# Down projections of two gated MLPs by seven block products instead of eight, with accumulating DMAs for some subtractions and sums

## The chip, the core and the metric

The kernel runs on one core of one Trainium2 chip. The metric is the time of one execution on the device in microseconds. The traces come from one profiled execution; its span runs from its first instruction to its last.

## The reference

A small decoder of two layers over 512 positions and 1024 channels, all in float32. Layer 0 mixes tokens with a gated DeltaNet, layer 1 with sliding-window attention. Each layer ends with the gated MLP that the change is about (`D_FF` is 2816):

```python
def conv_gated_mlp(hn, w_up, conv_w, conv_b, w_down):
    u = causal_dwconv(hn @ w_up, conv_w, conv_b)      # width 3, depthwise
    gate, val = jnp.split(u, 2, axis=-1)
    return (jax.nn.silu(gate) * val) @ w_down

def reference(x, ...):
    ...
    for layer in range(DEPTH):                          # DEPTH = 2
        h = h + (gated_deltanet(...) if layer < 1 else sliding_window_sink_attention(...))
        h = h + conv_gated_mlp(rmsnorm(h, ffn_norm_w[layer]), ffn_w_up[layer], ffn_conv_w[layer],
                               ffn_conv_b[layer], ffn_w_down[layer])
    return rmsnorm(h, final_norm_w)
```

## The kernel before

All large products are made from split operands: every float32 matrix x is cut into a high part (x rounded to the type that the matrix engine takes, `F32R`) and a low part x - high, and a product of 128x128 weights with 128x512 activations is three matmuls into one PSUM bank: high times high, high times low, low times high (`mm3`). PE is the matrix engine, DVE the vector engine, ACT the scalar engine, POOL and SP the two others; SP starts nearly all DMAs.

Channels lie on the 128 partitions and the 512 positions along the free dimension. The residual stream `h` is eight tiles of 128x512 in SBUF, two neighbours beside each other. Weights come by `load_stage`: one DMA on SP's queue brings up to eight 128x256 blocks into one of two `stage` buffers, and `cast` turns a 128-column half of them into weights, the high part by a copy on ACT (`whi`), the low part by a subtraction on DVE (`wlo`). There are three buffers of each.

`ffn` runs an MLP in two halves, channel tiles 0 to 11 and 12 to 21 of the 22. In a half's **up stage** each pair of channel tiles takes two stages (gate weights, value weights) and four `up` tiles of 24 matmuls each: gate 0, value 0, gate 1, value 1. What follows a tile is, on DVE and ACT: scaling out of PSUM, a scaled copy, two shifted multiply-adds (the convolution); for the gate a Silu; for the value the product with the gate, whose split gives the activations of the down projection. In the half's **down stage** there are eight output tiles m of 128 channels, two to a pair m2 and so to a pair of stages; each is 12 x 3 (then 10 x 3) matmuls of 128x512 into one bank of tag `d`, and DVE adds the bank to `h[m]`. The last output tile of all is made by `final` in two halves of 256 positions, between the last normalisation's pieces.

The program is written through a framework that gives buffers out and puts each engine's instructions into one order, by priority and by its own estimates; a table by hand sets the order of layer 0's token mixer, before the part that changes. Each engine then runs its list strictly in order, and waits where an operand or a buffer isn't ready. POOL has nothing to do in `ffn`, and issues no DMA in the kernel before.

Of the kernel before, what the change touches and what calls it, by code (L numbers as in the profile page):

```python
# [17 lines left out]
P = 128  # L18
T = 512
NC = T // P  # L20
D = 1024
KD = D // P
# [4 lines left out]
DFF = 2816  # L27
NF = DFF // P
# [13 lines left out]
def kernel(  # L42
# [26 lines left out]
    nc = tc.nc  # L69
    V, S, G, PE, SP = nc.vector, nc.scalar, nc.gpsimd, nc.tensor, nc.sync  # L70
# [6 lines left out]
    def nm(s):  # L77
        cnt[0] += 1
        return f"{s}_{cnt[0]}"

    wpool = ctx.enter_context(tc.tile_pool(name="weights", bufs=1, side="right"))
    psum = ctx.enter_context(tc.tile_pool(name="ps", bufs=1, space=PSUM))
    BANKS = {"d": 3, "g": 2, "s": 2, "p": 1}
    main = ctx.enter_context(tc.tile_pool(name="main", bufs=1))
# [13 lines left out]
        "o": 2,  # L98
        "p6s": 1,
        "gr": 1,  # L100
    }
# [12 lines left out]


    def load_stage(w, r0, kt, c0):
        st = wpool.tile([P, 8, 256], F32, tag="stage", bufs=2, name=nm("stage"))
        SP.dma_start(
            st[:, :kt, :],
            w[r0 : r0 + kt * P, c0 : c0 + 256].rearrange("(k p) c -> p k c", p=P),  # L120
        )
        return st

    def cast(st, kt, half, m=P):
        hi = wpool.tile([P, 8, P], F32R, tag="whi", bufs=3, name=nm("whi"))
        lo = wpool.tile([P, 8, P], F32R, tag="wlo", bufs=3, name=nm("wlo"))
        src = st[:, :kt, half * P : half * P + m]
        S.copy(hi[:, :kt, :m], src)  # L128
        V.tensor_tensor(lo[:, :kt, :m], src, hi[:, :kt, :m].bitcast(F32), op=ALU.subtract)  # L129
        return hi, lo  # L130

    def mm3(ps, w, kt, xh, xl, first=True, last=True, m=P):
        hi, lo = w
        for k in range(kt):
            PE.matmul(ps, hi[:, k, :m], xh[k], start=first and k == 0, stop=False)  # L135
            PE.matmul(ps, hi[:, k, :m], xl[k][:], start=False, stop=False)  # L136
            PE.matmul(ps, lo[:, k, :m], xh[k], start=False, stop=last and k == kt - 1)  # L137
# [16 lines left out]
    first = wpool.tile([P, 8, 256], F32, tag="stage", bufs=2, name=nm("stage"))  # L154
# [78 lines left out]
    st = [{} for _ in range(4)]  # L233
# [52 lines left out]
    gr = row("gr", F32R)[:, :]  # L286
# [56 lines left out]
    nk = const([P, 8, NC], s="nk")  # L343
# [369 lines left out]
    for i, line in enumerate(ORDER):  # L713
        for word in line.split():
            a, n = word[0], [int(d) for d in word[1:]]
# [22 lines left out]
        "rstd": ["p6s"],  # L738
        "qh": ["rq"],
        "ql": ["S"],  # L740
    }
# [15 lines left out]
    for h2 in range(HV // 2):  # L757
        a, b = wide("G"), wide("L")
# [6 lines left out]
    h4 = main.tile([P, 4, T], F32, tag="Xg", bufs=1, name="h4")  # L765
    h22 = [pair("pz") for _ in range(2)]
    hT = [h4[:, m, :] for m in range(4)] + [h22[m // 2][:, m % 2, :] for m in range(4)]
    for m in range(KD):
        xr = r2("hsq")
        x3 = xr[:].rearrange("p (c e) -> p c e", c=NC)  # L770
        SP.dma_start(x3, x[0, :, m * P : (m + 1) * P].rearrange("(c p) e -> p c e", p=P))
        pt = bank("g")
        for c in range(NC):
            PE.transpose(pt[:, c * P : (c + 1) * P], x3[:, c, :], ident[:])
        S.copy(hT[m], pt[:])
    for m2 in range(KD // 2):
        sts = [load_stage(a_w_out[0], 1024 * u, 8, 256 * m2) for u in range(2)]
        for j in range(2):
            m = 2 * m2 + j
            ps = bank("d")  # L780
            for u in range(2):
                w = cast(sts[u], 8, j)
# [4 lines left out]
    def rstd_cols(h):  # L787
# [13 lines left out]
        V.reciprocal(rt[:], rt[:])  # L801
        return rt

    def rstd_rows(h):
        rt = rstd_cols(h)
        dg = r2("sum")
# [12 lines left out]
    def normed(h, off):  # L819
        xh, xl = [], []  # L820
        for k in range(KD):
            a, b = r2("xh", F32R), r2("xl", F32R)
            split_scaled(h[k], norm_c[:, off + k : off + k + 1], a, b)
            xh.append(a)
            xl.append(b)
        return xh, xl


    def ffn(l, h, last=False):
        wup, wdn = ffn_w_up[l], ffn_w_down[l]  # L830
        uh, ul = normed(h, NFFN + 8 * l)
        rs = rstd_rows(h)

        def tap(j, t):
            i = j * 2 * NF + t
            return fcw[l][:, i : i + 1] if i < 128 else onw_c[:, 4 * l + i - 128 : 4 * l + i - 127]

        def up(w, t, tag):
            ps = bank("d")
            mm3(ps[:], w, KD, uh, ul)  # L840
            u = r2("u")
            V.tensor_tensor(u[:], ps[:], rs[:], op=ALU.mult)  # L842
            acc = r2(tag)
            b = CB + 2 * NF * l + t
            S.activation(acc[:], u[:], AF.Identity, bias=norm_c[:, b : b + 1], scale=tap(2, t))  # L845
            for d in (1, 2):
                V.scalar_tensor_tensor(  # L847
                    acc[:, d:], u[:, : T - d], tap(2 - d, t), acc[:, d:], op0=ALU.mult, op1=ALU.add
                )
            return acc  # L850

        for t0, t1 in ((0, 12), (12, 22)):
            gh, gl = [], []
            for t in range(t0, t1, 2):
                if l == 0 and t == 6:
                    bias_rows()
                sg = load_stage(wup, 0, 8, t * P)
                sv = load_stage(wup, 0, 8, DFF + t * P)
                gp, lp = wide("G"), wide("L")
                for j in range(2):  # L860
                    a = up(cast(sg, 8, j), t + j, "ga")
                    S.activation(a[:], a[:], AF.Silu)  # L862
                    b = up(cast(sv, 8, j), NF + t + j, "va")
                    V.tensor_tensor(b[:], a[:], b[:], op=ALU.mult)
                    split(b[:], gp[:, j, :], lp[:, j, :])
                    gh.append(gp[:, j, :])
                    gl.append(lp[:, j, :])
            ku = (t1 - t0) // 2
            for m2 in range(KD // 2):
                sts = [load_stage(wdn, (t0 + u * ku) * P, ku, 256 * m2) for u in range(2)]  # L870
                for j in range(2):
                    m = 2 * m2 + j
                    ws = [cast(sts[u], ku, j) for u in range(2)]
                    if last and t1 == NF and m == KD - 1:
                        final(h, lambda ps, ts, u: down(ps, ws, ku, gh, gl, ts, u))
                        continue
                    ps = bank("d")
                    for u in range(2):
                        down(ps[:], ws, ku, gh, gl, slice(0, T), u)
                    V.tensor_tensor(h[m], h[m], ps[:], op=ALU.add)  # L880

    def down(ps, ws, ku, gh, gl, ts, u):
        us = slice(u * ku, u * ku + ku)
        a, b = [t[:, ts] for t in gh[us]], [t[:, ts] for t in gl[us]]
        mm3(ps, ws[u], ku, a, b, first=u == 0, last=u == 1)

# [67 lines left out]
    def attention(h):  # L954
# [173 lines left out]
```

## Time and profile before

| | |
|---|---|
| median of 3 runs | 1457.99 us (1455.2 to 1465.97) |
| profiled execution | 1458.21 us, its span 1456.4 us |
| mean granted clock of PE | 0.996 |
| busy in the span | PE 98%, weight loads 80%, DVE 65%, ACT 49%, POOL 1% |
| DMA | 152.71 MB, 105 GB/s on average |

"Busy" is a share of the whole span, and the stages differ. PE's matmuls overlap their neighbours by design, so that the time from start to start, not the duration of one, says what a matmul costs. The profile's waits name what an engine waited for; the idle time of an engine that nobody waits for costs nothing. Lines (L137) are those of the kernel before where a row is of it, and of the changed kernel in rows of the changed program.

### The profile page before, as it was taken

The numbers are of one execution on the slowest core, as the hardware profiler recorded it, in microseconds if no ns is written. First come the engines' busy times: TensorE is split into PE (matmuls) and PEld (weight loads), VectorE is DVE, ScalarE is ACT, GpSimd is POOL, SyncE is SP. The second block draws the span as 40 slices with busy tenths as digits, with TensorE's granted clock in tenths as the row PEclk, the third lists the DMA queues.
The fourth block names the chain that finished last, engine by engine and source line by source line (L and its number), as shares of the span: only waits on it lengthen the run. The fifth ranks groups of instructions, "written<-read, shape, count | busy, mean of one in ns | idle before, by whom it ended". The sixth has DMA issues, their size and how long they took to land.

```text
span 1456.4 us, 19545 instructions
## 1 busy us (share of the span) xinstructions
PE 1432.3 (98%) x7519; PEld 1163.6 (80%) x7519; DVE 953.5 (65%) x1661; ACT 718.9 (49%) x1406; POOL 20.1 (1%) x47
## 2 busy tenths in 40 slices
PE   7999999999999999999999999999999999999998
PEld 5778877888877788888888888877788888888887
DVE  5896885978844436776247765777757774366754
ACT  7764564656646424443224444578744443234433
POOL 1000000000000000000010000000000000000000
PEclk9999999999999999999999999999999999999999
DMA  5334254163366523232232234221132322322222
GB/s 154 92 99 112 78 171 119 59 189 110 98 189 209 163 87 108 69 114 87 87 116 91 83 95 130 89 79 44 58 105 69 116 83 86 122 87 87 94 73 94
DMA packets 163074, 152.71 MB, mean 105 GB/s; under 512 B 24165, under 2 KB 150694, under 8 KB 162982
## 3 DMA queue, kind: packets, MB, share of 16 engines
q1 hardware_dynamic: 160722, 151.27, 33.3%
q8 instruction: 59, 0.97, 0.3%
q10 hardware_dynamic: 2259, 0.20, 0.2%
q14 instruction: 34, 0.27, 0.1%
HBM read 134.65 MB, written 16.80 MB: 104 GB/s over the span
## 4 chain that ended last, share of the span: by engine, by line
PE 95%; DMA 3%; ACT 1%; DVE 1%; issue 0%; ACTq 0%; DVEq 0%; SPq 0%
PE d L135 27%; PE d L137 27%; PE d L136 26%; PE s L585 2%; PE p L1043 1%; PE s L600 1%; PE g L1038 1%; PE s L625 1%; PE p L608 1%; PE s L562 1%; PE p L555 1%; PE s L1013 1%; PE g L450 1%; PE g L671 1%; PE g L375 1%; DMA ol<-od 0%
## 5 line engine op out<-in xcount | busy, mean ns | idle before, releaser
L135 PE MATMUL d<-xh,whi 128*128 128x512 f32 x1192 | 475.8, 400 | 0.1
L137 PE MATMUL d<-xh,wlo 128*128 128x512 f32 x1192 | 473.3, 398 | 0.0
L136 PE MATMUL d<-xl,whi 128*128 128x512 f32 x1192 | 471.6, 396 | 0.0
L128 ACT CAST whi<-stage 128x1024 fp32r<-128x1024 f32 (+2 forms) x236 | 230.5, 979 | 337.6 <-PE d L136 318.6
L129 DVE TENSOR_TENSOR wlo<-stage,whi 128x1024 fp32r<-128x1024 f32 (+2 forms) x236 | 267.3, 1133 | 120.4 <-ACT whi L128 114.3
L137 PEld LDWEIGHTS d<-xh,wlo 128*128 128x128 f32 x1192 | 224.4, 188 | 50.5 <-issue 1.4
L136 PEld LDWEIGHTS d<-xl,whi 128*128 128x128 f32 x1192 | 224.3, 188 | 48.2 <-issue 1.2
L135 PEld LDWEIGHTS d<-xh,whi 128*128 128x128 f32 x1192 | 224.7, 188 | 46.1 <-issue 0.7
L842 DVE TENSOR_TENSOR sz<-d,p6s 128x512 f32<-128x512 f32 x58 | 40.0, 689 | 62.9 <-PE d L137 61.0
L227 DVE SCALAR_TENSOR_TENSOR acc<-d,cwc,acc 128x511 f32<-128x511 f32 (+2 forms) x96 | 70.7, 740 | 9.3 <-ACT acc L224 8.8
L862 ACT ACTIVATE dt<-dt 128x512 f32<-128x512 f32 x44 | 27.8, 632 | 83.5 <-DVE dt L847 83.5
L135 PE MATMUL d<-sy,whi 128*128 128x512 f32 (+1 forms) x148 | 57.6, 390 | 0.0
L137 PE MATMUL d<-sy,wlo 128*128 128x512 f32 (+1 forms) x148 | 57.5, 389 | 0.0
L135 PE MATMUL d<-kT,whi 128*128 128x512 f32 (+1 forms) x146 | 57.5, 396 | 0.0
L136 PE MATMUL d<-sy,whi 128*128 128x512 f32 (+1 forms) x148 | 57.0, 385 | 0.0
L137 PE MATMUL d<-kT,wlo 128*128 128x512 f32 (+1 forms) x146 | 57.0, 390 | 0.0
L136 PE MATMUL d<-qT,whi 128*128 128x512 f32 (+1 forms) x146 | 56.8, 389 | 0.0
L847 DVE SCALAR_TENSOR_TENSOR va<-sz,fcw,va 128x511 f32<-128x511 f32 (+1 forms) x58 | 43.4, 748 | 2.7 <-ACT va L845 1.7
L847 DVE SCALAR_TENSOR_TENSOR dt<-sz,fcw,dt 128x511 f32<-128x511 f32 (+1 forms) x58 | 43.4, 748 | 1.2 <-ACT dt L845 0.2
L842 DVE TENSOR_TENSOR zl<-d,p6s 128x512 f32<-128x512 f32 x30 | 20.7, 689 | 33.4 <-PE d L137 33.1
L507 DVE TENSOR_TENSOR sT<-sT,p6s 64x31 f32<-64x31 f32 (+15 forms) x124 | 40.9, 330 | 2.0
L501 DVE TENSOR_TENSOR p6s<-sN,sT 64x31 f32<-64x31 f32 (+15 forms) x124 | 40.9, 330 | 1.8
(377 smaller groups left out, 2116.8 us busy)
## 6 DMA issues: line engine op xcount, KB each, us to landing
stage<-in_ffn_w_up_dram SPq DMA_DIRECT2D x44, 1024.0 KB, 5.1
stage<-in_a_w_in_dram SPq DMA_DIRECT2D x23, 1024.0 KB, 5.4
stage<-in_ffn_w_down_dram SPq DMA_DIRECT2D x16, 768.0 KB, 4.3
stage<-in_ffn_w_down_dram SPq DMA_DIRECT2D x16, 640.0 KB, 4.1
stage<-in_a_w_out_dram SPq DMA_DIRECT2D x8, 1024.0 KB, 5.0
zd<-sz SPq DMA_DIRECT2D x16, 256.0 KB, 2.1
od<-o SPq DMA_DIRECT2D x16, 256.0 KB, 2.5
stage<-in_b_w_q_dram SPq DMA_DIRECT2D x4, 1024.0 KB, 5.0
```

Source lines behind the costliest of these rows:

```text
L128: S.copy(hi[:, :kt, :m], src)
L129: V.tensor_tensor(lo[:, :kt, :m], src, hi[:, :kt, :m].bitcast(F32), op=ALU.subtract)
L135: PE.matmul(ps, hi[:, k, :m], xh[k], start=first and k == 0, stop=False)
L136: PE.matmul(ps, hi[:, k, :m], xl[k][:], start=False, stop=False)
L137: PE.matmul(ps, lo[:, k, :m], xh[k], start=False, stop=last and k == kt - 1)
L227: V.scalar_tensor_tensor(acc[:, d:], ps[:, : T - d], col, acc[:, d:], op0=ALU.mult, op1=ALU.add)
L501: V.tensor_tensor(tv, N[:, s, s + 1 : 32].unsqueeze(2).to_broadcast([64, n, m]), Tm[:, s : s + 1, 0:m].to_broadcast([64, n, m]), op=ALU.mult,)
L507: V.tensor_tensor(Tm[:, s + 1 : 32, 0:m], Tm[:, s + 1 : 32, 0:m], tv, op=ALU.subtract)
L585: PE.matmul(x[:, si], t[:, i, cs], S0[:, si], start=True, stop=True)
L842: V.tensor_tensor(u[:], ps[:], rs[:], op=ALU.mult)
L847: V.scalar_tensor_tensor(acc[:, d:], u[:, : T - d], tap(2 - d, t), acc[:, d:], op0=ALU.mult, op1=ALU.add)
L862: S.activation(a[:], a[:], AF.Silu)
```

## The change

It has three parts.

**Seven products.** A pair of output tiles (m, m+1) and a pair of channel tiles (f0, f1) with the positions in two halves of 256 make a product of 2x2 blocks. `seven_products` computes it from seven block products instead of eight, by sums of blocks taken ahead (the scheme of Strassen and Winograd). On the side of the activations `forms` makes four sums for each pair of channel tiles and splits f1, a half of f0 and the four sums into high and low parts, kept in rows that other parts of the program have left, three new rows of tag `f`, and `form_rows` hands them out. On the side of the weights each stage gets four sums of 128 x (3 x 128) or 128 x (2 x 128) elements, in place in the stage, and 3 casts of the whole width and one of the half (`cast`, `cast_to`). The matmuls are 128x256. Four products of a pair m2 collect in banks a, b, c, d, are added to `h` from there, two of them (a and d) collect a further product each and are added once more, one of these into three quarters of the pair at once, and the seventh (bank e) into two quarters. A down stage's stages are split into parts u = 0 (three channel pairs) and u = 1 (three, or two in the second half). The first two pairs m2 are interleaved: part 0 of both, then part 1 and the rest of the first, then of the second. The last pair m2 of the whole kernel stays as it was, eight products, with `final`.

**A third stage.** `down_stage` takes turns among the two `stage` buffers and a third one of its own (`st3`, 128 x 6 x 256), which also serves `rstd_rows`.

**Accumulating DMAs.** The low part of the value weights in the up stages (22 of the 44 weight tiles of a layer) is no longer made by DVE: ACT writes -high into the `wlo` buffer with one more instruction, and a DMA issued by POOL adds the weights to it from DRAM (`cast_added`). The first of the four sums of each down stage is made the same way, by a DMA that adds one block of the stage's weights from DRAM to another (`G.dma_start(A21, ...)`). There are 44 of the first kind (128 x 8 x 128 floats, 512 KB in pieces of 512 bytes) and 30 of the second (192 or 128 KB). The space that POOL keeps for the DMAs' descriptors is cut from its default to 4096 bytes a partition.

```diff
+    def cast_added(st, src, half):
+        hi, lo = weights()
+        hs = slice(half * P, half * P + P)
+        S.copy(hi[:], st[:, :, hs])
+        S.activation(lo[:], hi[:].bitcast(F32), AF.Copy, scale=-1.0)
+        G.dma_start(lo[:], src[:, :, hs], accum_op=ALU.add)
+        return hi, lo
...
+    def cast_to(w, at, src):
+        n = src.shape[1]
+        hi, lo = [t[:, at : at + n, :] for t in w]
+        S.copy(hi, src)
+        V.tensor_tensor(lo, src, hi.bitcast(F32), op=ALU.subtract)
...
                 for j in range(2):
                     a = up(cast(sg, 8, j), t + j, "ga")
                     S.activation(a[:], a[:], AF.Silu)
-                    b = up(cast(sv, 8, j), NF + t + j, "va")
+                    b = up(cast_added(sv, tiles_of(wup, 0, 8, DFF + t * P), j), NF + t + j, "va")
                     V.tensor_tensor(b[:], a[:], b[:], op=ALU.mult)
-                    split(b[:], gp[:, j, :], lp[:, j, :])
...
+                sevens.append(forms(*f, rows, plain))
...
+                sts = [down_stage(src) for src in srcs]
+                if not (plain and m2 == KD // 2 - 1):
+                    todo.append(seven_products(sts, srcs, parts, sevens, h_pairs[m2], m2 % 2))
+                    if m2 == 1:
+                        for i in (0, 1, 0, 0, 1, 1):
+                            next(todo[i])
...
+    def forms(f0, f1, rows, plain):
+        B11, B12, B21, B22 = f0[:, HALF[0]], f0[:, HALF[1]], f1[:, HALF[0]], f1[:, HALF[1]]
+        ta, tb = r2("Ta"), r2("Tb")
+        V.tensor_tensor(ta[:, HALF[0]], B12, B11, op=ALU.subtract)
+        V.tensor_tensor(ta[:, HALF[1]], B22, ta[:, HALF[0]], op=ALU.subtract)
+        V.tensor_tensor(tb[:, HALF[0]], B22, B12, op=ALU.subtract)
+        V.tensor_tensor(tb[:, HALF[1]], B21, ta[:, HALF[1]], op=ALU.subtract)
...
+    def seven_products(sts, srcs, parts, sevens, hp, odd):
...
+        a, b, d, c = [bank(t)[:, 0:256] for t in ("d", "g", "s", "d" if odd else "p")]
+        for u in range(2):
+            A11, A12, A21, A22 = blocks(u)
+            nk, end = len(parts[u]), u == 1
+            G.dma_start(A21, srcs[u][:, 1 : 2 * nk : 2, P : 2 * P], accum_op=ALU.add)
+            w = cast(sts[u], 2 * nk, 0)
+            product(a, w, 0, "B11", u)
...
+            product(b, w, 1, "B21", u)
...
+            V.tensor_tensor(A11, A21, A11, op=ALU.subtract)
+            V.tensor_tensor(A12, A12, A11, op=ALU.subtract)
+            w = cast(sts[u], 2 * nk, 1)
+            product(d, w, 0, "T1", u)
...
+            product(c, w, 1, "T4", u)
...
+            V.tensor_tensor(A22, A22, A11, op=ALU.subtract)
+            yield
+        e = bank("p" if odd else "g")[:, 0:256]
+        w4 = weights()
+        for u in range(2):
+            w = cast(sts[u], 2 * len(parts[u]), 0)
+            product(a, w, 0, "T2", u, first=False)
+            product(d, w, 1, "B22", u, first=False)
+            cast_to(w4, 4 * u, blocks(u)[3])
...
-    nc = _bacc.Bacc("TRN2", target_bir_lowering=False, num_devices=1)
+    nc = _bacc.Bacc("TRN2", target_bir_lowering=False, num_devices=1, dynamic_dma_scratch_size=4096)
```

Three places show how the order of the instructions changes.

**ACT in an up stage**, first half of layer 0, at the value weights of a pair's first tile. Before: the high part's copy (L128), the scaled copy of an earlier tile (L845), Silu (L862), the next gate weights.

```order
L128 CAST whi_5527<-stage_5487 128x1024
L845 ACTIVATE dt_5442<-sz_5440,normc_101,fcw_371 128x512
L862 ACTIVATE dt_5442<-dt_5442 128x512
L128 CAST whi_5565<-stage_5485 128x1024
L845 ACTIVATE va_5478<-zl_5476,normc_101,fcw_371 128x512
```

In the changed program stand there:

```order
L137 CAST whi_5552<-stage_5514 128x1024
L870 ACTIVATE dt_5453<-sz_5451,normc_101,fcw_371 128x512
L138 ACTIVATE wlo_5553<-whi_5552 128x1024
L889 ACTIVATE dt_5453<-dt_5453 128x512
L129 CAST whi_5589<-stage_5512 128x1024
```

The negated high part (L138) is new. It stands behind the scaled copy of an earlier tile (L870), which waits for DVE's scaling of that tile; the DMA on POOL can start only after L138.

**DVE where the first down stage begins**, after the last up tile (its product with the gate is L864 before, L891 now). Before: low parts of the weights of two stages and the sums into `h` (L880).

```order
L864 TENSOR_TENSOR va_6105<-dt_6069,va_6105 128x512
L141 TENSOR_TENSOR at_5963<-va_6105,at_5962 128x512
L129 TENSOR_TENSOR wlo_6167<-stage_6114,whi_6166 128x768
L880 TENSOR_TENSOR h_4560<-h_4560,d_6124 128x512
L129 TENSOR_TENSOR wlo_6213<-stage_6208,whi_6212 128x768
L129 TENSOR_TENSOR wlo_6217<-stage_6210,whi_6216 128x768
L880 TENSOR_TENSOR h_4560<-h_4560,d_6170 128x512
```

Now stand there the three remaining sums of the activations (L955 to L957), their four splits (L961), a sum of weights in the third stage (L1034), and then the first low part of the weights of part 1 (`wlo_6311`):

```order
L891 TENSOR_TENSOR va_6172<-dt_6135,va_6172 128x512
L130 TENSOR_TENSOR wlo_6287<-st_1017_6201,whi_6286 128x768
L955 TENSOR_TENSOR o_6177<-va_6172,o_6177 128x256
L956 TENSOR_TENSOR rq_6178<-va_6172,va_6099 128x256
L957 TENSOR_TENSOR rq_6178<-va_6172,o_6177 128x256
L961 TENSOR_TENSOR f_6184<-va_6172,f_6183 128x512
L961 TENSOR_TENSOR f_6187<-va_6099,f_6187 128x256
L961 TENSOR_TENSOR m_1013_6191<-o_6177,gr_6190 128x512
L961 TENSOR_TENSOR acc_6194<-rq_6178,m_1013_6191 128x512
L1034 TENSOR_TENSOR st_1017_6201<-st_1017_6201 128x3x128
L130 TENSOR_TENSOR wlo_6311<-stage_6199,whi_6310 128x768
```

All of L955 to L961 is ahead of `wlo_6311` in DVE's queue, so that PE's part 1 waits for it.

**DVE at the second pair of the down stage**, part 1, whose weights lie in `stage_6203`. Before, DVE at such a place had two low parts and one sum, as in the rows above. Now:

```order
L130 TENSOR_TENSOR wlo_6435<-stage_6203,whi_6434 128x768
L1011 TENSOR_TENSOR h_4560<-h_4560,g_6361 128x512
L1025 TENSOR_TENSOR stage_6203<-stage_6203 128x3x128
L1011 TENSOR_TENSOR h_4560<-h_4560,d_6257 128x256
L1026 TENSOR_TENSOR stage_6203<-stage_6203 128x3x128
L1011 TENSOR_TENSOR h_4560<-h_4560,g_6258 128x256
L130 TENSOR_TENSOR wlo_6461<-stage_6203,whi_6460 128x768
```

L1025 takes the sum that the accumulating DMA makes in `stage_6203`. The additions of two banks to `h` (L1011), L1026 and the next low part of weights are queued behind it.

More of the change, by code (lines that the diff above doesn't have):

```diff
@@ L100 @@
         "gr": 1,
+        "f": 3,
     }
@@ L740 @@
         "ql": ["S"],
+        "Ta": ["o"],
+        "Tb": ["rq"],
     }
@@ L850, in up @@
             return acc
-        for t0, t1 in ((0, 12), (12, 22)):
-            gh, gl = [], []
+        for t0, t1 in ((0, 12), (12, NF)):
+            plain = last and t1 == NF
+            rows = form_rows()
+            sevens = []
             for t in range(t0, t1, 2):
@@ new lines, with form_rows, parts, halves @@
+    HALF = [slice(0, 256), slice(256, 512)]
+    def form_rows():
+        for _ in range(len(YROLE)):
+            w = wide("G")
+            yield w[:, 0, :]
+            yield w[:, 1, :]
+        for tag in ("S", "S", "us", "f", "f", "f", "gr"):
+            yield row(tag, F32R)[:]
+        w = pair("m32", F32R)
+        yield w[:, 0, :]
+        yield w[:, 1, :]
+        yield row("acc", F32R)[:]
+    def forms(f0, f1, rows, plain):
[5 more added lines that the diff above has]
+        V.tensor_tensor(tb[:, HALF[1]], B21, ta[:, HALF[1]], op=ALU.subtract)
+        def parts(src, hi, lo):
+            S.copy(hi, src)
+            V.tensor_tensor(lo, src, hi.bitcast(F32), op=ALU.subtract)
+            return hi, lo
+        def halves(names, w):
+            return {n: [t[:, HALF[i]] for t in w] for i, n in enumerate(names)}
+        w1 = parts(f1[:], next(rows), next(rows))
+        out = {"f1": w1, **halves(("B21", "B22"), w1)}
+        if plain:
+            out["f0"] = parts(f0[:], next(rows), next(rows))
+            out.update(halves(("B11",), out["f0"]))
+        else:
+            r = next(rows)
+            out["B11"] = parts(B11, r[:, HALF[0]], r[:, HALF[1]])
+        out.update(halves(("T1", "T2"), parts(ta[:], next(rows), next(rows))))
+        out.update(halves(("T3", "T4"), parts(tb[:], next(rows), next(rows))))
+        return out
```

97 lines of the change are left out of this document (73 added, 24 removed).

## The prediction

> **What bounds the kernel now.** I read the page's head, its shares and its chain of waits first, then the busy time of each engine by stretches.
>
> ```profile
> span 1456.4 us, 19545 instructions
> PE 1432.3 (98%) x7519; PEld 1163.6 (80%) x7519; DVE 953.5 (65%) x1661; ACT 718.9 (49%) x1406; POOL 20.1 (1%) x47
> ...
> PE 95%; DMA 3%; ACT 1%; DVE 1%; issue 0%; ACTq 0%; DVEq 0%; SPq 0%
> ```
>
> The profiled execution took 1458.2 us, 1.8 us more than its span and 0.2 us from the median of the three runs, so the sum below is made against 1458.2. The chain that ended last is PE for 95%. The first row below is an up stage (layer 0, first half), the second the down stage behind it, the third a stretch of layer 1; columns are PE, PE's weight loads, DVE, ACT and POOL busy, then the granted clock.
>
> ```profile
> 553.00:684.00 131.00, 131.00 (x571) 106.62 (x570) 93.38 (x120) 58.75 (x73) 0.00 (x0) 1.00 0.28 87
> 684.00:750.00 66.00, 66.00 (x290) 54.13 (x290) 23.55 (x28) 14.55 (x17) 2.36 (x5) 1.00 0.33 104
> 1200.00:1300.00 100.00, 100.00 (x438) 82.07 (x437) 45.73 (x56) 28.02 (x34) 0.00 (x0) 1.00 0.30 98
> ```
>
> PE never idles in the MLPs, at full clock. DVE is busy 71% of the up stage and 36% of the down stage. So only two things count: how much PE time goes, and whether a wait opens on PE where there is none. 438 matmuls of 128x512 in 100 us is one per 0.2283 us.
>
> **What the seven products save on PE.** `final` runs 128x256 matmuls of the same kind today. The rows are the second of them and the last, 43 steps on:
>
> ```profile
> 1439.68 0.28 PE L136 MATMUL d<-nt,whi 128*128 128x256 f32 x1
> ...
> 1444.74 0.28 PE L137 MATMUL d<-kT,wlo 128*128 128x256 f32 x1
> ```
>
> 5.06 us / 43 = 0.1177 us, a little more than half of 0.2283. Before, 22 x 8 x 3 x 2 = 1056 matmuls belong to the down stages; the last pair's 60 stay, so 996 x 0.2283 = 227.4 us change. After, a pair m2 has 7 products x 6 (or 5) channel pairs x 3 matmuls: 4 x 126 and 4 x 105 in layer 0, 4 x 126 and 3 x 105 in layer 1, 1743 x 0.1177 = 205.2 us. **Saved: 22.2 us**, at most.
>
> **What DVE gets in a down stage.** Durations by shape (mean ns):
>
> ```profile
> L129 DVE TENSOR_TENSOR wlo<-stage,whi 128x768 fp32r<-128x768 f32 x32 | 30.7, 958 | 38.1 <-ACT whi L128 38.0
> L880 DVE TENSOR_TENSOR h<-h,d 128x512 f32<-128x512 f32 x16 | 11.0, 690 | 34.1 <-PE d L137 34.1
> L129 DVE TENSOR_TENSOR wlo<-gst,whi x1: 548/548/548, 18.2 to 18.2; 128x384 fp32r<-128x384 f32 x1
> L940 DVE TENSOR_TENSOR pz<-pz,d 128x256 f32<-128x256 f32 x2 | 0.8, 422 | 3.1 <-PE d L137 3.1
> L847 DVE SCALAR_TENSOR_TENSOR va<-sz,fcw,va 128x510 f32<-128x510 f32 x29 | 21.8, 751 | 1.0
> ```
>
> Neighbours overlap a little, as starts in the timeline show:
>
> ```profile
> 676.23 0.69 DVE L842 TENSOR_TENSOR zl<-d,p6s 128x512 f32<-128x512 f32 x1 [0.27 <-PE d L137]
> 676.87 0.96 DVE L129 TENSOR_TENSOR wlo<-stage,whi 128x768 fp32r<-128x768 f32 x1
> 677.81 1.54 DVE L847 SCALAR_TENSOR_TENSOR dt<-zl,fcw,dt 128x511 f32<-128x511 f32 x2
> ```
>
> So 512 elements cost 0.64 us, 768 cost 0.94, and with the same 0.05 off, 384 cost 0.50 and 256 cost 0.37. A pair m2 of a first half needs six low parts of 768, two of 384, six sums of 384 (the DMAs make the other two), five additions of 256 to `h`, one of 768, one of 512: 5.64 + 4.00 + 1.85 + 0.94 + 0.64 = 13.1 us, against 126 x 0.1177 = 14.8 us of PE. In a second half it is 11.7 against 12.4 us. Before it was about 5 us against 16.4. DVE has become nearly as long as PE, and the cover is thin wherever something comes late. I followed the changed order by hand at the first down stage; zero is the time at which PE could go on behind the last up matmul.
>
> *The beginning.* PE's result reaches DVE 0.2 us later than PE itself can go on (0.43 us from the start of a matmul to the addition that waits for it, less 0.23):
>
> ```profile
> 1430.71 0.39 PE L137 MATMUL d<-at,wlo 128*128 128x512 f32 x1
> ...
> 1431.14 0.69 DVE L880 TENSOR_TENSOR pz<-pz,d 128x512 f32<-128x512 f32 x1 [2.03 <-PE d L137]
> ```
>
> Then come, in DVE's queue up to `wlo_6311`: the scaling 0.64, a low part 0.94, two multiply-adds with a weight sum behind each 2.50, the product 0.64, a low part 0.94, three sums 1.11, four splits 2.29, a weight sum 0.50, and `wlo_6311` 0.94: 10.5, so it is there at 10.7 us. PE has part 0 of two pairs to do, 72 matmuls, and 8 high ones of part 1: 9.4 us. **PE waits 1.3 us** (none before: there a split of 0.69 us was all).
>
> *The second pair's part 1.* `stage_6203` reuses the buffer of `stage_6197`, whose last reader on DVE stands 5.4 us of work behind `wlo_6311`, at 16.1 us. Then the load, ACT's copy and DVE's low part:
>
> ```profile
> stage<-in_ffn_w_down_dram SPq DMA_DIRECT2D x16, 768.0 KB, 4.3
> acc<-in_x_dram SPq DMA_DIRECT2D x8, 256.0 KB, 2.9
> stage<-in_a_w_in_dram SPq DMA_DIRECT2D x2, 512.0 KB, 6.2
> stage<-in_ffn_w_up_dram SPq DMA_DIRECT2D x44, 1024.0 KB, 5.1
> ...
> L128 ACT CAST whi<-stage 128x768 fp32r<-128x768 f32 x32 | 26.8, 836 | 84.2 <-PE d L136 84.2
> L128 ACT CAST whi<-stage 128x1024 fp32r<-128x1024 f32 x172 | 180.4, 1052 | 193.0 <-PE d L136 178.4 <-DMA stage<-in_a_w_in_dram 4.2 <-issue 4.0
> L845 ACT ACTIVATE dt<-sz,normc,fcw 128x512 f32<-128x512 f32 x29 | 23.7, 817 | 0.8 <-DVE sz L842 0.6
> ```
>
> 16.1 + 4.3 + 0.84 + 0.94 = 22.2 us, while PE has finished the first pair and four matmuls near 21 us: **1.4 us** of waits with the small ones on the way. The accumulating DMA starts when the load has landed, at 20.4, and takes L_d; L1025 waits for it, and behind L1025 stand two additions, L1026 and `wlo_6461`, 2.7 us: 23.1 + L_d. PE is there at 24.8: it waits L_d - 1.7. Later pairs have 2 us or more in hand.
>
> *L_d* isn't in the trace: POOL issues no DMA. Nearest is the 256 KB row above, whose pieces are of 512 bytes too, 2.9 us; 192 KB would be 2.7. The destination is read as well, which at the 0.8 us that 256 KB more cost between the 768 and 1024 KB rows is 0.6; I add 0.3 for the writing of descriptors. Value 3.8, bounds 2.7 and twice 2.9. **So 2.1 us**, and 0.2 at the end of that pair: 5.0 us a down stage, **20 us for four**; one us of L_d more costs 4. The last pair of the kernel, whose weights queue behind the sums, gets 1.6 us.
>
> **What the up stages get.** DVE loses a low part of 1024 for each value tile, and gains the sums and more splits, in all within 1 us of the same per pair. No cover goes there: PE waited for nothing. ACT gains an instruction of 1.05 us, with 45% busy before. The new thing is the chain to the low part. Its buffer comes free when the tile three back is done; PE then has two tiles of 24 and two high matmuls to do, 50 x 0.2283 = 11.4 us. For the second value tile of a pair, DVE reaches the scaling that L870 waits for only 2.1 us after that (the sums and splits of the last pair stand in front), L870 takes 0.82 and L138 1.05, so the DMA goes off at 4.0 and has 7.4 us. The first value tile has 8.3. POOL's queue is in order, but the stage's sum in front of the last value tile is loaded long before.
>
> The DMA's duration, L_u, is the price that decides. The row of the same size and the same pieces, 512 KB of `in_a_w_in`, took 6.2 us; reading the destination too adds 1.6 at the rate above, descriptors 0.3: 8.1 us. Bounds: 2.9 (the 256 KB row) and twice 6.2 = 12.4. In each of 22 pairs of tiles PE waits for L_u less 7.4, once: 0.7 x 22 = **15 us**. By the Trainium skill, DMA: Bandwidth & Descriptors, section Anatomy of one DMA, a DMA that POOL issues takes 2.0 us plus its bytes at 436 GB/s, which for 512 KB would be an estimate of 3.2 us: no wait in the up stages, and a sum of 1458. The trace speaks against it only by the plain 6.2 us, and can't show the accumulation.
>
> **The sum:** 1458.2 - 22.2 + 20 + 1.6 + 15.4 = **1473 us**.
>
> **The rivals.**
> *The DMAs stay under their cover.* L_u of 7.4 or less: 1458, with L_d at its lower bound 1453, no change. For it: the 6.2 us row was taken with other loads in flight at the kernel's start, and 1024 KB land in 5.1. Against it: every reason above adds to the plain time.
> *The down stages hide their chains (faster).* If a stage's 5 us shrink to 1, as they would if ACT and DVE pieces overlap better than my list by hand and L_d is under 2.7, and L_u is under 7.4, it is 1442. For it: DVE's sums stay below PE's in every pair. Against: the 10.7 us chain is made of rows, and PE's cover there is 9.4 at most.
> *The up-stage DMAs are long (much slower).* With L_u at 12.4, (12.4 - 7.4) x 22 = 110 us in place of 15: 1568. It begins to decide at 9.5 us, 1504. POOL has to write some thousand descriptors for a DMA of 1024 pieces, which no row shows. By the Trainium skill, SBUF — State Buffer, section SBUF: two separate sides, DVE instructions that use two ports lock POOL out of writing descriptors, and a DMA of 0.62 us took 3.1; with 2.5 us more L_u it would be 1528 here. The rows of DVE in these stages are TENSOR_TENSOR and SCALAR_TENSOR_TENSOR, and that page has no two-port mode for the first.
> That the change doesn't do what it says, seven products and DMAs in place of DVE, is not open: the order has them.
>
> **How the numbers follow.** Forecast (L_u between 7.4 and 9.5, 1460 to 1504): 36%. Under cover, 1453 to 1460: 32%. Faster: 12%. Long DMAs: 20%. The range leaves out half of the faster case and the worst of the long one, where L_u is above 12: **1445 to 1562**. About 1%, 14.6 us, is what a measurement can tell from no change. Faster by over 1%: 12%. Within: the case under cover and the forecast's lower end, 37%. Slower: 51%.
>
> **What would show it.** PE's 128x256 matmuls at 0.118 us apart; PE waiting in up stages for DMA on `wlo` before every second value tile, none if L_u is below 7.4; the landing times of POOL's DMAs of 512 and 192 KB against 8.1 and 3.8; in each down stage one wait of about 1.3 us for DVE's `wlo` at the first part 1, and 2 us behind a DMA into a stage at the second pair. I am wrong if these DMAs are much shorter or longer, or if PE waits in the later pairs, where DVE's 13.1 of 14.8 us should be enough.

## The result, and the profile after

The changed kernel takes 1500.72 us (median of 4 runs, 1496.8 to 1504.46), the kernel before 1456.6: a ratio of 1.0285 (95% interval 1.0241 to 1.0329), 44 us slower by the medians. Its profiled execution has a span of 1502.5 us, 46.1 more than before. The page's head, shares and chain:

```profile
span 1502.5 us, 21864 instructions
PE 1438.9 (96%) x8266; PEld 1197.8 (80%) x8266; DVE 1059.1 (70%) x1974; ACT 810.1 (54%) x1554; POOL 126.6 (8%) x121
...
PE 83%; DMA 7%; DVE 5%; ACT 2%; issue 2%; DVEq 0%; POOL 0%; POOLq 0%; ACTq 0%; SPq 0%
```

PE's share of the chain has gone from 95 to 83%, and DMA and DVE have come in. The stages show where. The rows are, in this order, the first half of layer 0 (up, down), its second half (up, down), layer 1's mixer, and the second up stage of layer 1; columns as in the prediction.

```profile
556.45:691.77 135.32, 134.68 (x589) 109.24 (x588) 95.55 (x144) 72.31 (x96) 21.09 (x14) 1.00 0.70 146
691.77:757.45 65.68, 62.31 (x505) 60.88 (x504) 52.20 (x90) 25.80 (x36) 7.61 (x6) 0.97 0.46 120
757.45:880.53 123.08, 112.51 (x482) 91.55 (x481) 77.81 (x115) 58.85 (x77) 18.15 (x12) 0.96 0.63 129
880.53:939.57 59.04, 52.81 (x421) 50.03 (x420) 52.01 (x99) 30.43 (x49) 10.13 (x14) 1.00 0.40 104
939.57:1114.05 174.48, 171.54 (x932) 131.08 (x931) 126.60 (x318) 118.02 (x303) 5.69 (x9) 0.98 0.22 71
...
1313.34:1434.29 120.95, 112.45 (x483) 91.79 (x482) 78.00 (x115) 59.06 (x77) 19.44 (x13) 0.96 0.64 129
```

The same stretches of the kernel before:

```profile
547.07:681.52 134.45, 134.45 (x589) 109.32 (x588) 95.01 (x122) 59.58 (x76) 0.00 (x0) 1.00 0.29 91
681.52:747.45 65.93, 65.93 (x290) 54.09 (x289) 23.90 (x28) 15.16 (x19) 0.00 (x0) 1.00 0.33 104
747.45:857.31 109.86, 109.86 (x481) 90.14 (x480) 76.13 (x96) 46.61 (x59) 6.26 (x12) 1.00 0.29 93
857.31:912.25 54.94, 54.94 (x242) 45.07 (x241) 30.48 (x41) 22.18 (x32) 2.08 (x4) 1.00 0.38 117
912.25:1080.24 167.99, 167.99 (x932) 128.73 (x930) 123.45 (x313) 115.84 (x299) 0.00 (x0) 1.00 0.23 71
```

The first up stage, with twelve accumulating DMAs, loses 0.9 us; the second, with ten, loses 13.2. The down stages of the first halves come out even, that of layer 0's second half loses 4.1, and layer 1's mixer, whose instructions the change doesn't touch, loses 6.5. PE's waits from 480 us on, the longest in total (before, all of them together were under 1 us):

```profile
PE d L156 <- DMA wlo<-in_ffn_w_up_dram: 19.2, 3, 10.0
PE s L1006 <- ACT whi L129: 7.9, 4, 2.4
PE d L1008 <- DVE wlo L130: 6.0, 9, 1.0
PE g L796 <- DVE va L691: 2.8, 1, 2.8
PE d L154 <- ACT whi L129: 1.9, 1, 1.9
```

Only 3 of the 44 low parts made by DMA were waited for, two of them for 10.0 and 8.5 us. Both are the first value tile of a second half; the experiments call this place the entry. (The third wait, 0.6 us, is in layer 0's first half, behind a DMA that took 8.9 us.) The timeline at the entry of layer 0, engine by engine (SP, ACT, POOL, PE):

```profile
750.51 14.76 SPq L119 DMA_DIRECT2D stage<-in_ffn_w_up_dram  x4
760.66 1.05 ACT L137 CAST whi<-stage 128x1024 fp32r<-128x1024 f32 x1 [3.29 <-DMA stage<-in_ffn_w_up_dram]
761.61 1.05 ACT L129 CAST whi<-stage 128x1024 fp32r<-128x1024 f32 x1
762.56 1.06 ACT L138 ACTIVATE wlo<-whi 128x1024 fp32r<-128x1024 f32 x1
764.08 1.59 POOL L139 DMA_DIRECT2D wlo<-in_ffn_w_up_dram  x1 [17.93 <-PE d L156]
775.95 1.56 POOL L139 DMA_DIRECT2D wlo<-in_ffn_w_up_dram  x1 [10.29 <-issue]
765.22 0.40 PE L155 MATMUL d<-xl,whi 128*128 128x512 f32 x1
775.66 0.79 PE L156 MATMUL d<-xh,wlo 128*128 128x512 f32 x1 [10.04 <-DMA wlo<-in_ffn_w_up_dram]
776.25 0.63 PE L154 MATMUL d<-xh,whi 128*128 128x512 f32 x1
```

SP can issue the up stage's first load only at 750.5, 6.9 us before that stage begins at 757.5 (its first matmul). In the kernel before it was 732.8, 14.7 us ahead. The second load, of the value weights, goes out 4.4 us ahead in place of 10.5. The rows are SP in the kernel before, and what SP waited for before 750.5 in the changed one:

```profile
732.79 22.83 SPq L118 DMA_DIRECT2D stage<-in_ffn_w_up_dram  x4
...
SPq L119 <- DVE wlo L149: 11.8, 1, 11.8
```

L149 makes the low part of the weights for the seventh product, the last reader of a stage buffer. In layer 1 the gate weights come in time, and the value weights wait for L149 in the same way: their load goes out 7.3 us ahead in place of 10.5. There POOL's queue adds to it: L138 ends at 1314.4, but the DMA goes off at 1315.8, behind the DMA of a down stage's sum that had waited for its load until 1315.0.

At the entry of layer 0 the value weights land at 760.6, ACT's queue puts another copy in front of L138, and the DMA goes off at 764.1. It takes 11.5 us in place of its median of 6.4, and PE stands from 765.6 to 775.7. PE reached this tile 1.5 us after the DMA went off, so that 5 us of the 10.0 are the lateness, and 5 us that the DMA took 11.5 us and not 6.4. Then PE's matmuls are 0.43 us apart in place of 0.228, until 779.7: the granted clock has been halved.

```profile
770.00:780.00 10.00, 4.34 (x10) 3.46 (x11) 0.00 (x0) 0.00 (x0) 1.56 (x1) 0.50 0.81 133
```

That is 9 matmuls at 0.2 us more, 1.8 us on top of the wait. The Trainium skill (TensorE: Matmul & The Clock Gate, Part 1) describes this: the clock is halved after an idle window of about 3.4 us and comes back after a busy one. The trace agrees, with the granted clock of 0.50 and about 4 us of slow matmuls.

The accumulating DMAs themselves, KB each and median us to landing, then the spread of all 44 of the first kind (the other 15 and 8 are those of 192 KB):

```profile
wlo<-in_ffn_w_up_dram POOLq DMA_DIRECT2D x44, 512.0 KB, 6.4
stage<-in_ffn_w_down_dram POOLq DMA_DIRECT2D x15, 192.0 KB, 4.2
st<-in_ffn_w_down_dram POOLq DMA_DIRECT2D x8, 192.0 KB, 3.9
...
DMA to landing us min/median/max: 6.1/6.4/12.2
```

### The profile page after: what moved, and what is told of

The parts are those of the page before. It is cut to its first block, busy times and chain, and to the rows that moved or that the text cites. A ratio compares the mean times of both kernels' runs of the same rounds, so it can differ in the third digit from the quotient of the medians.

```text
span 1502.5 us, 21864 instructions
## 1 busy us (share of the span) xinstructions
PE 1438.9 (96%) x8266; PEld 1197.8 (80%) x8266; DVE 1059.1 (70%) x1974; ACT 810.1 (54%) x1554; POOL 126.6 (8%) x121
## 4 chain that ended last, share of the span: by engine, by line
PE 83%; DMA 7%; DVE 5%; ACT 2%; issue 2%; DVEq 0%; POOL 0%; POOLq 0%; ACTq 0%; SPq 0%
PE d L156 20%; PE d L154 20%; PE d L155 20%; DMA wlo<-in_ffn_w_up_dram 2%; DVE wlo L130 2%; PE s L604 1%; DMA stage<-in_ffn_w_down_dram 1%; PE d L1008 1%; PE p L1207 1%; PE s L619 1%; PE d L1006 1%; PE g L1202 1%; PE d L1007 1%; PE s L1008 1%; PE s L644 1%
## 5 line engine op out<-in xcount | busy, mean ns | idle before, releaser
L156 PE MATMUL d<-xh,wlo 128*128 128x512 f32 x1192 | 479.2, 403 | 20.7 <-DMA wlo<-in_ffn_w_up_dram 19.2
L155 PE MATMUL d<-xl,whi 128*128 128x512 f32 x1192 | 476.9, 401 | 0.0
L129 ACT CAST whi<-stage 128x1024 fp32r<-128x1024 f32 (+2 forms) x192 | 183.2, 958 | 243.2 <-PE d L155 158.0
L130 DVE TENSOR_TENSOR wlo<-stage,whi 128x1024 fp32r<-128x1024 f32 (+2 forms) x192 | 212.2, 1108 | 67.8 <-ACT whi L129 67.1
L139 POOL DMA_DIRECT2D wlo<-in_ffn_w_up_dram x44 | 69.8, 1587 | 651.0 <-ACT wlo L138 602.8
L867 DVE TENSOR_TENSOR sz<-d,p6s 128x512 f32<-128x512 f32 x58 | 40.0, 689 | 63.5 <-PE d L156 61.2
L137 ACT CAST whi<-stage 128x1024 fp32r<-128x1024 f32 x44 | 46.1, 1049 | 42.9 <-PE d L155 37.6
L138 ACT ACTIVATE wlo<-whi 128x1024 fp32r<-128x1024 f32 x44 | 46.2, 1051 | 0.2
L129 ACT CAST whi<-st 128x768 fp32r<-128x768 f32 (+1 forms) x30 | 23.7, 791 | 32.7 <-DMA st<-in_ffn_w_down_dram 10.4
L1017 POOL DMA_DIRECT2D stage<-in_ffn_w_down_dram x20 | 25.1, 1253 | 167.6 <-DMA stage<-in_ffn_w_down_dram 67.2
```

The costliest lines, as they stand in the source:

```text
L137: S.copy(hi[:], st[:, :, hs])
L138: S.activation(lo[:], hi[:].bitcast(F32), AF.Copy, scale=-1.0)
L139: G.dma_start(lo[:], src[:, :, hs], accum_op=ALU.add)
```

## The experiments

All were profiled, and compared with the kernel before on the same chip. The first table has their times, the second what the profiled execution of each spent in each stage, from the first matmul of a stage to the first of the next (us).

| | median us | ratio to before (95%) |
|---|---|---|
| changed | 1500.72 | 1.0285 (1.0241 to 1.0329) |
| the same again (e10) | 1498.41 | 1.0296 (1.0269 to 1.0324) |
| e1, two first value tiles on DVE | 1474.12 | 1.0126 (1.0090 to 1.0161) |
| e3, first down sums on DVE | 1473.2 | 1.0103 (1.0062 to 1.0145) |
| e4, no accumulating DMA | 1456.14 | 0.9989 (0.9976 to 1.0002) |
| e5, before + DMAs in the up stages | 1456.99 | 1.0006 (0.9982 to 1.0029) |
| e8, two loads held back | 1488.26 | 1.0207 (1.0180 to 1.0233) |
| e6, e4 + third stage last | 1456.2 | 0.9982 (0.9964 to 1.0000) |
| e9, e6 + one pair by eight products | 1450.14 | 0.9957 (0.9942 to 0.9972) |

| stage | before | changed | e10 | e1 | e3 | e4 | e5 | e8 | e6 | e9 |
|---|---|---|---|---|---|---|---|---|---|---|
| start to the first up tile | 547.1 | 556.5 | 544.6 | 543.5 | 554.5 | 549.7 | 544.2 | 545.6 | 544.8 | 553.6 |
| layer 0, up, first half | 134.4 | 135.3 | 134.4 | 135.4 | 134.9 | 134.4 | 134.4 | 135.1 | 134.4 | 134.4 |
| down, first half | 65.9 | 65.7 | 64.6 | 64.4 | 63.5 | 62.8 | 65.9 | 66.0 | 62.2 | 62.1 |
| up, second half | 109.9 | 123.1 | 122.4 | 111.2 | 118.9 | 110.8 | 109.9 | 118.6 | 109.9 | 109.9 |
| down, second half | 54.9 | 59.0 | 61.1 | 59.8 | 54.1 | 53.9 | 54.9 | 61.6 | 54.1 | 55.6 |
| layer 1's mixer | 168.0 | 174.5 | 174.7 | 174.3 | 173.9 | 173.9 | 168.0 | 174.7 | 174.0 | 168.0 |
| layer 1, up, first half | 133.7 | 133.7 | 133.7 | 133.7 | 133.7 | 133.7 | 133.7 | 133.7 | 133.7 | 133.7 |
| down, first half | 65.9 | 65.6 | 65.2 | 65.8 | 62.1 | 62.1 | 65.9 | 65.7 | 62.1 | 62.1 |
| up, second half | 109.9 | 121.0 | 124.8 | 111.6 | 115.8 | 109.9 | 109.9 | 118.8 | 109.9 | 109.9 |
| down and end | 66.7 | 68.2 | 71.0 | 69.8 | 66.1 | 66.0 | 66.7 | 68.7 | 66.1 | 66.1 |
| first up tile to the end | 909.3 | 946.1 | 951.9 | 926.1 | 923.0 | 907.6 | 909.4 | 942.9 | 906.3 | 901.8 |

**e1: the first value tile of each second half on DVE.**

```diff
-b = up(cast_added(sv, ..., j), NF + t + j, "va")
+early = t == 12 and j == 0
+wv = cast(sv, 8, j) if early else cast_added(sv, ..., j)
+b = up(wv, NF + t + j, "va")
```

> The changed kernel, but the low part of the first value tile of each MLP's second half (t = 12, j = 0, two tiles in the program) is again made by DVE; the other 42 stay with the accumulating DMA. Theory A (entries): in the up stages the DMAs cost time only where a second half begins, because there the value weights land late and the DMA then shares the DMA engines with the next stage's load (12 us for 6.4). The two waits of 10.0 and 8.5 us and the slow clock behind them, about 2.3 us each, go: 1500 - 23 = 1477 us, and both second up stages come back to about 110 us. Theory B (everywhere): the 28 MB more of DMA traffic and POOL's work slow the program in many places, and the waits only move to the second value tile: 1492 or more.

1474.12 us, and the second up stages 111.2 and 111.6 us: two of 44 DMAs cost nearly all that the up stages lost (1.3 and 1.7 us are left). The entry is the place, as theory A said; theory B is out.

**e3: the first sum of the down stages on DVE.**

```diff
-G.dma_start(A21, srcs[u][:, 1 : 2 * nk : 2, P : 2 * P], accum_op=ALU.add)
 w = cast(sts[u], 2 * nk, 0)
+V.tensor_tensor(A21, A21, A22, op=ALU.add)
```

> The changed kernel, but the first sum of each down stage (30 sums) is made by DVE, behind the first low part of its stage, and not by an accumulating DMA. Theory A: the wait of PE at the second pair's part 1 (1.9, 2.0, 1.6 and 2.4 us in the four down stages), which ACT's copy of the sum passes on, and the slow clock behind it (about 2 us) go: 12 to 15 us less, 1486 us. Rival (DVE is full): DVE gets 30 x 0.5 = 15 us more in stages where it is already 0.8 busy, so that as much is lost in waits for the low parts as is gained: 1500 us or more.

1473.2 us, twice the gain that was expected. In the second pair of a down stage of the changed kernel one sees the wait that theory A named (the rows are of POOL, DVE and PE):

```profile
711.93 1.27 POOL L1017 DMA_DIRECT2D stage<-in_ffn_w_down_dram  x1 [28.61 <-DMA stage<-in_ffn_w_down_dram]
716.07 0.56 DVE L1025 TENSOR_TENSOR stage<-stage 128x384 f32<-128x384 f32 x1 [2.31 <-DMA stage<-in_ffn_w_down_dram]
716.96 0.38 PE L1006 MATMUL s<-ktok,whi 128*128 128x256 f32 x1 [1.88 <-ACT whi L129]
```

That wait is gone in e3, and the four down stages together are 12.7 us shorter (258.5 to 245.8 by the table), close to the expected. The rest was not expected: without the sums' DMAs the last pair lets go of its buffers sooner (the up stage's first load is issued at 744.6, 8.3 us ahead of the stage, in place of 6.9), at layer 1's entry no sum stands in front in POOL's queue, and the waits at the entries fell too:

```profile
PE d L156 <- DMA wlo<-in_ffn_w_up_dram: 7.0, 3, 4.7
```

The sum on DVE did not make DVE the bound.

**e4: no accumulating DMA.** e3 with `cast` in place of `cast_added` everywhere.

> The changed kernel without any accumulating DMA: seven products and the third stage alone, all low parts and all sums on DVE. Theory A: the gains of the two other runs add up: 1500 - 23 - 14 = 1463 us, with up stages of 134 and 110 us as in the kernel before. Rival (DVE is full): in the up stages DVE had 71% before and gets the sums and splits beside its old low parts, and the waits for it make 1480 us or more.

1456.14 us, no different from before, and 7 us less than theory A's sum. The up stages are back to 134.4, 110.8, 133.7 and 109.9 us with all low parts on DVE, so DVE had room for them beside the new sums and splits. PE's waits from 480 us on, the first rows:

```profile
PE d L1008 <- DVE wlo L130: 3.6, 6, 1.0
PE d L154 <- ACT whi L129: 3.6, 2, 3.1
PE d L1006 <- ACT whi L129: 1.2, 3, 0.6
PE s L1008 <- DVE wlo L130: 1.1, 3, 0.4
```

So the DMAs cost 38.5 us from the first up tile on (946.1 less 907.6), and the seven products with the third stage alone gain 1.7 us of the 22.2 that PE has less to do. The four down stages are 8.6 us shorter than before. They lose the other 13.6 us in themselves: the rows with L1008 and L1006, 5.9 us of waits for weights, are theirs. Layer 1's mixer takes back 5.9 us, and the second up stage of layer 0 0.9.

**e5: the kernel before with the DMAs of the up stages alone.**

```diff
-b = up(cast(sv, 8, j), NF + t + j, "va")
+b = up(cast_added(sv, ..., j), NF + t + j, "va")
```

> The kernel before, with eight products as they were, and only the 44 low parts of the value weights by accumulating DMA (and the same space for descriptors as in the changed kernel). Theory A: the same entries show: two waits of about 9 us and the slow clock behind them, 1457 + 22 = 1479 us, nothing elsewhere. Theory B (everywhere): 1490 us or more. A third possibility: without the seven products the stage's buffers come free earlier at the entry, and the waits are half as long: 1467 us.

1456.99 us, and each stage as before. No theory had this. At its second up stage's beginning (744.5 us), SP and POOL:

```profile
729.85 43.54 SPq L118 DMA_DIRECT2D stage<-in_ffn_w_up_dram  x6
742.91 1.56 POOL L138 DMA_DIRECT2D wlo<-in_ffn_w_up_dram  x1 [76.08 <-ACT wlo L137]
...
DMA to landing us min/median/max: 6.2/6.5/7.4
```

The load is issued 14.6 us ahead of the stage, the DMA goes off before the stage begins, and none of the 44 takes over 7.4 us. The DMAs alone cost nothing. What differs at this place in the changed kernel is that the seven products read each stage buffer until the end of a pair, so that the loads behind it come late (SP's wait for L149 above).

**e8: the next loads held back at the entry.** POOL copies one element of the first low part into each of the next two stage buffers, so that their loads wait until the DMA has landed.

```diff
+def hold(c):
+    st = wpool.tile([P, 8, 256], F32, tag="stage", bufs=2, name=nm("stage"))
+    G.tensor_copy(st[:, 0, 0:1], first_lo[:, 0, 0:1].bitcast(F32))
+    SP.dma_start(st[:], tiles_of(wup, 0, 8, c + (t + 2) * P))
+    return st
...
```

> The changed kernel, but where a second half begins, the two stage loads of the next pair of channel tiles (t = 14) are held back until the accumulating DMA of the first value tile has landed: POOL copies one element of the low part into each stage buffer first. Theory (shared DMA engines): that DMA took 11.5 and 12.2 us in place of 6.4 because these two loads of 1024 KB ran beside it. Alone it takes 6.4 us, and the two waits of PE fall from 10.0 and 8.5 to about 5 and 3 us: 10 us less than the changed kernel, 1490 us. Rival (the DMA is long for a reason of its own at that place, such as work queued on POOL or engines writing to SBUF): it still takes 11 to 12 us and nothing changes, 1500 us.

1488.26 us. POOL and PE at the first entry, then POOL at the second:

```profile
753.40 1.59 POOL L139 DMA_DIRECT2D wlo<-in_ffn_w_up_dram  x1 [18.15 <-PE d L156]
760.19 0.30 POOL L889 COPY stage<-wlo 128x1 f32<-128x1 f32 x2 [5.20 <-DMA wlo<-in_ffn_w_up_dram]
759.98 0.80 PE L156 MATMUL d<-xh,wlo 128*128 128x512 f32 x1 [5.06 <-DMA wlo<-in_ffn_w_up_dram]
...
1305.62 1.26 POOL L1030 DMA_DIRECT2D st<-in_ffn_w_down_dram  x1 [19.80 <-DMA st<-in_ffn_w_down_dram]
1306.38 2.12 POOL L139 DMA_DIRECT2D wlo<-in_ffn_w_up_dram  x1
1313.57 0.79 PE L156 MATMUL d<-xh,wlo 128*128 128x512 f32 x1 [6.46 <-DMA wlo<-in_ffn_w_up_dram]
```

Without the two loads, the DMAs take 6.6 and 7.2 us from issue to PE's next matmul, not 11.5 and 12.2: the loads beside them made them long, as the theory said. The waits fell from 10.0 and 8.5 to 5.1 and 6.5 us. What is left is lateness. At the second entry it was more than expected, and there the DMA of a down stage's sum (L1030, here for the next down stage's first load) stands in front in POOL's queue, as it does in the changed kernel, and waits for that load until 1305.6. The two second up stages are 6.7 us shorter together; from the first up tile on, e8 is 3.2 and 9.0 us shorter than the two profiled executions of the changed kernel. The 12 us between the medians can't be placed closer than that.

**e6: e4 with the third stage last in every half.**

```diff
-if turns[0] % 3 == 0:
+if (turns[0] - 1) % 8 + 1 in (2, 5, 8):
```

> As the kernel without accumulating DMAs (e4, 1456 us), but the third stage takes the 2nd, 5th and 8th stage of every half, in place of every third one of the whole program, so that it always holds the last stage and both ordinary buffers come free earlier at the end of a half. Theory: the 6 us that the start of layer 1's mixer lost in all these kernels (a wait of 3.1 us for the copy of weights that landed late, and the slow clock behind it) go, and 1 us where layer 0's second half begins: 1450 us. Rival: the buffers are held as long, since the last stages are read to the end, and the place of the third stage doesn't matter: 1456 us.

1456.2 us. The second up stage is back to 109.9 us, but the mixer is as long as in e4, 174.0 us. The load came a little sooner (issued 3.4 us ahead of the mixer in place of 2.5), but PE still waits 2.1 us for ACT's copy and 1.2 us for DVE's low part. The theory was wrong on the mixer.

**e9: e6 with the last pair of layer 0's second half by eight products.**

```diff
-plain = last and t1 == NF
+plain = t1 == NF
```

The diff shows one line; the second output tile of that pair is also made like the first where `final` doesn't follow.

> As e6 (1456.2 us), but in layer 0 too the last pair of output tiles of the second half is made by eight products of 128x512, as it is in layer 1. Theory: the 6 us lost at the start of layer 1's mixer come from DVE, which is still at the last pair's additions and low parts when the mixer needs its first weights; eight products need 1.3 us more on PE, but less than half of DVE's work there, so that most of the 6 us come back: 1452 us. Rival: the wait is for the weights of the mixer, whose load comes late whatever DVE does, and the pair only costs its 1.3 us: 1457 us.

1450.14 us: faster than the kernel before by 0.43% (interval 0.28 to 0.58). The first 113 us of the mixer:

```profile
915.52:1028.25 112.73, 112.73 (x643) 85.57 (x642) 86.82 (x230) 83.54 (x219) 0.00 (x0) 1.00 0.24 77
```

The pair costs 1.5 us (54.1 to 55.6), and the mixer is back to 168.0 us, with PE busy without a gap in its first 113 us. By the stages e9 is 4.5 us shorter than e6 (906.3 to 901.8); the intervals of the two ratios still overlap. The first 5 us of the mixer, in e6 and in e9:

```profile
905.33:910.33 5.00, 1.81 (x8) 0.86 (x6) 5.00 (x9) 3.59 (x5) 4.07 (x8) 1.00 0.22 77
915.52:920.52 5.00, 5.00 (x27) 4.17 (x26) 3.18 (x5) 3.72 (x5) 0.00 (x0) 1.00 0.63 210
```

In e6 DVE is busy all the time and PE 1.8 us of 5; in e9 PE is busy all the time and DVE 3.2 us. The load of the mixer's second weights also went out sooner in e9, 11.3 us ahead in place of 3.4. So the loss came from this pair, by its work on DVE or its hold on the stage buffers; one run doesn't say how much was which.

**e10: the changed kernel once more.**

> The changed kernel once more, unchanged. Its profiled execution was 9.4 us behind the kernel before already at the first up tile, where both programs issue the same instructions; kernels run since then had that point between 543 and 555 us. Theory (scatter of the clock's dips in layer 0's mixer): the point lies somewhere between 543 and 557 us again, while the stages behind it repeat to within 2 us: 123, 59, 121 and 68 us for the second up stage, the second down stage, the last up stage and the end. Rival (the change itself slows the mixer): the point is at 555 us or later again.

1498.41 us. The first up tile starts at 544.6 us, not at 556.5: the 9.4 us that the first profile lost before the MLPs are scatter. The rows are 340 to 344 us of the kernel before and of the first profile of the changed one:

```profile
340.00:344.00 4.00, 4.00 (x29) 3.56 (x28) 4.00 (x7) 2.17 (x4) 0.00 (x0) 1.00 0.23 36
340.00:344.00 4.00, 4.00 (x22) 3.04 (x21) 1.53 (x3) 1.46 (x4) 1.09 (x2) 0.50 0.15 25
```

In this execution the clock fell to half in a stretch of small matmuls, where the other had all of it from 320 to 352 us (0.84 on average in this one). Not all stages repeat to within 2 us: the last up stage took 124.8 us for 121.0, the second down stage 61.1 for 59.0, and the end 71.0 for 68.2. The waits at the entries were 9.8 and 12.0 us this time, behind DMAs of 11.3 and 13.5 us.

## Why the prediction was wrong

The sum was 15 us above the profiled time of before; the medians are 44 apart. From the first up tile on, the first profile lost 36.7 us and the second 42.6. By the prediction's own terms, in the first profile:

- *PE's saving, -22.2 us.* Right. The 128x256 matmuls are 0.1177 us apart where nothing waits, 504 of them 59.3 us, and what a down stage takes beyond that are waits.
- *Four down stages, +20 + 1.6 us, so -0.6 with the saving.* Measured +5.0 with it. For the first halves 64.5 us was forecast each (65.9 less the saving of 6.4, and 5.0): 65.7 and 65.6, 64.6 and 65.2 in e10. The single waits came as predicted: 0.9 us for 1.3 at the first low part of part 1, and 1.9 us for 2.1 behind the DMA of the second pair's sum, with an L_d of 4.2 or 3.9 us for the 3.8 assumed. (2.7, 0.6 and 0.3 us, from which L_d was added up, make 3.6, not 3.8, and with it 19.2 us for four stages, not 20.) The 1.9 us were a wait for ACT's copy of the sum; DVE's queue behind the sum, which the prediction followed, added a wait of 0.07 us. Not in the sum was that the clock can fall behind such a cluster of waits:

```profile
720.00:724.00 4.00, 4.00 (x28) 4.00 (x28) 2.65 (x5) 1.46 (x3) 0.00 (x0) 0.76 0.27 87
```

  The second half of layer 0 was undersized: 9.6 us beyond its 420 matmuls (49.4 us), where 5.0 were put. DVE is busy 52 of its 59 us, and there are eight waits of 0.2 to 2.0 us.
- *The up stages, 0.7 us in each of 22 pairs, 15.4 us.* Measured 25.2 us: of the right order by chance, and **wrong in both parts**. L_u is 6.4 us, not 8.1, and so under the cover, the time from the DMA's start to PE's need: in the steady state there is no wait, and that rival was right there. The 0.3 us that L_u and L_d had for descriptors is in no run a figure of its own. By the Trainium skill's rule that the prediction weighed (DMA: Bandwidth & Descriptors, section Anatomy of one DMA) the estimate was 3.2 us; the measurement decides, at twice that. The step that failed is the cover: 7.4 and 8.3 us were worked out from the buffer three tiles back, for a pair in the middle of a stage, and used for every pair. In the middle they hold: from the DMA's issue to PE's first use the trace has 7.7 to 8.9 us there. Where a second half begins, a load of the stage is late, so that the cover is 1.5 us in layer 0 and 3.7 in layer 1, and the DMA runs beside two loads of 1024 KB and takes 11.5 and 12.2 us. The prediction had also set POOL's queue aside, since the sum in front of a value tile "is loaded long before"; in layer 1 it was not, which is 1.4 us of the lateness. Two waits and the slow clock behind them make most of the 13.2 and 11.1 us that these up stages lose. e5 shows that the DMA alone doesn't do it, e8 that the shared transfer is about half of the wait at the first entry, e1 that these two tiles are nearly all of it.
- *Layer 1's mixer, not in the sum.* 6.5 us. The prediction followed the order by hand at the first down stage and not past the last one. The last pair's work reaches into the mixer: e9 shows that it is this pair, and not whether by DVE's low parts and additions or by the late hold on the buffers.
- *Start to the first up tile.* 9.4 us of the first profile, -2.5 in the second: scatter.

"Later pairs have 2 us or more in hand" held for the first halves, where no later pair waits, and not for the second. The rival with long DMAs put its price on all 22 pairs, and none of the rivals had the entry as a place of its own.

## What to carry to other kernels

A cover that is worked out from the steady state doesn't hold at the seams: follow the first item of a stage from the moment its buffer comes free, through every queue, to the wait. Who holds a buffer longer delays a load two stages on, and an operation that got longer by a few us in a place with slack (e5) becomes a wait where the slack has gone. And a scheme that saves PE time by giving DVE more pays only where DVE has room: taking one of the fifteen pairs back to eight products turned no change (e6) into 0.4% faster.

## What the runs showed of the hardware

- An accumulating DMA of 512 KB in pieces of 512 bytes takes 6.4 us in the median; it took 8.9 and 9.4 us beside one load of 1024 KB and one of 768 KB, and 11.5 and 12.2 us beside two of 1024 KB. With those two held back it took 6.6 and 7.2 us (e8).
- POOL is busy for 1.57 us with each of these DMAs (median; 1.56 to 2.12 over the 44). Of the rule in the Trainium skill (SBUF — State Buffer, SBUF: two separate sides) that DVE can lock POOL out, which the prediction's rival drew on, these runs show nothing.
- At the entries POOL sent the second DMA of 512 KB only when the first had landed (in layer 0 issued at 775.95, landed at 775.6, ready since 766.5, and marked "issue"); in both executions of the changed kernel, at both entries, it went out 0.3 us behind the landing. One of 192 KB and one of 512 KB went out 0.8 us apart. Whether the space for descriptors, cut to 4096 bytes, is the reason wasn't tried.
- Short waits close together can be enough to lose the clock: in the first down stage waits of 0.3, 0.3 and 1.9 us stand within 5 us, none is longer, and it fell to 0.76 over 4 us. It does not always: in the down stage of layer 0's second half, behind waits of 0.2 and 2.0 us within 4 us, it stayed at 1.00.
- A wait costs PE some 0.3 us more than is listed, since the profile counts it from the modelled end of the matmul before. In e4's first down stage, at full clock, the matmul behind a listed wait of 0.55 us starts 0.83 us after the one before it, and the next 0.23 us later, where 0.1177 is the spacing.
